# The second part of a hybrid attention layer in the order of a written list: pair scores and four-head values in one run, heads permuted

## The chip, the cores and the metric

The kernel runs on one core of a Trainium2 chip. The metric is the device time of one execution in microseconds (us). The kernel before took 233.28 us (median of three runs, 233.16 to 233.49).

The engines are TensorE (PE in the profile; its weight loads stand apart as PEld), VectorE (DVE), ScalarE (ACT), GpSimd (POOL) and SyncE (SP), which here issues the transfers. Each has its own instruction queue, and they wait for one another through semaphores.

## The reference

One decoder layer on a sequence of 256 tokens of width 1024, in float32. Two attention branches run beside each other, both with eight heads: MLA (branch a: low-rank queries, keys and values; 64 + 32 dimensions per head, the 32 with a rotary key that all heads share) and MoBA (branch b: 64 dimensions per head; with 256 tokens there is only one block, so it is causal attention). Cut to what matters:

```python
mod = silu(c) @ w_ada + b_ada
shift, scale, gate = split(mod, 3)
h = rms_norm(x, g_pre) * (1 + scale) + shift
(q_lat, kv_lat, k_rope, z_mla, q_mb, k_mb, v_mb, z_mb, merge_logits) = split_cols(h @ w_in)
q = rms_norm(q_lat, g_q_lat) @ w_uq              # 8 heads of 64 + 32
kv = rms_norm(kv_lat, g_kv_lat) @ w_ukv          # 8 heads of 64 + 64
q_full, k_full = concat(q_nope, rope(q_pe)), concat(k_nope, broadcast(rope(k_rope)))
o_mla = causal_attention(q_full, k_full, v_mla)
y_mla = (o_mla * silu(z_mla)) @ w_o_mla
o_mb = causal_attention(rope(q_mb), rope(k_mb), v_mb)
y_mb = (o_mb * silu(z_mb)) @ w_o_moba
g_a, g_b = split(sigmoid(merge_logits + b_merge))
y = (g_a * y_mla + g_b * y_mb) @ w_out
out = x + gate * rms_norm(y, g_post)
```

## The kernel before

**Split operands.** Every large matrix product is done with operands cut in two: a rounded high part (`w1`, an ACT copy to float32r) and the rest (`w2`, a DVE subtraction of `w1` from the raw weights, L266 in the profile for both, as the helper `free` is recorded). A product is three matmuls: high by high, high by low, low by high. Weights arrive by DMA in five raw buffers of 1 MB (`RAW`), are cut in pieces of 512 columns by `split_one` (L251), and wait in a ring of five pairs `w1`, `w2` of 1024 columns (`RING`). `pump` (L238) issues the next load on SP as soon as a raw buffer is free.

**First stage**, to about 57.7 us: x is normalized, transposed and modulated to `h1` + `h2`, and MoBA's queries, keys and values are projected. Its order is written out by hand: the strings START, STEP and LAST (L44 to L46) are read token by token (`tokens`, L391), and `ordered` (L78) chains each instruction to the one before on its engine. The helper makes all of it L82 in the profile.

**Second part**, from `lat_mm` on. What the steps are:

- `lat_mm` (L525 to L527): the latent projection, 48 matmuls of 416 columns; `lat_stats`, `lat_evac`, `lat_tr` norm and transpose it. `lat_tr` also copies the shared rotary key to all heads, two copies on POOL and one on DVE (L571).
- `moba_rope`, `moba_tr`: rotary embedding of MoBA's q and k (products on DVE L463 and L466, sums on POOL L467) and their transposes.
- `F` (L431), called "filler": one of 24 projections of 128 output columns (the merge gates and the two SiLU gates), 24 matmuls of 256 columns each (L441 to L443), then a tanh on ACT. A raw buffer feeds two fillers.
- `uq_*`, `ukv_*`, `qpe_tr`: MLA's queries, keys and values from the latents.
- `scores` (L656): q·k for a MoBA pair of heads or one MLA head. A MoBA head has 64 dimensions, so its matmuls use 64 rows of the array, the upper or the lower half; the first query block takes one matmul of 128 columns (L669), the second three of 256 (L677). The softmax follows on DVE and ACT.
- `p_tr` (L696): three transposes of the probabilities, and ACT's copy `pT`.
- `pv` (L705): the values of two heads. Each head writes 64 columns of the array: one matmul of 256 columns (L710) and one of 128 (L714), two passes each. Then u, the product with the SiLU gate, and its cut in two.
- `oproj` (L762): the output projections of a branch, 8 per branch, 12 matmuls each, and the merge `yy` with the gates; for branch a POOL subtracts to get the low part `y2` (L781).
- `ada_gate` (L728): the residual gate, summed on DVE over eight weight tiles 1024 wide (L736, L738), and a bias added on POOL (L741).
- `out_mm`, `out_part` (L866 to L907): the last projection in seven pieces, the post-norm and the stores.

These are called in program order, with `fill` putting one to eight fillers or `oproj("b", m)` between the attention steps. The order on each engine is then decided by the framework's scheduler, which simulates the program and gives each engine the instruction that it finds ready; only first-stage instructions are chained by hand. Splits of coming weights are called by `split_ahead` whenever a ring slot is released.

Of the kernel before, what the change touches and what calls it, by code (L numbers as in the profile page):

```python
# [34 lines left out]
HEAD = 213  # L35
LOADS = "a00 a01 w00 w01 a10 a11 " + " ".join(f"w{j}0 w{j}1 a{j + 1}0 a{j + 1}1" for j in range(1, 7)) + " w70 w71 m"
# [9 lines left out]
LAST = "P0v P1v P2v V P0q P0k P1q P2q P1k P2k"  # L46
POOL_LOW = []
# [15 lines left out]
def hybrid_layer_kernel(ctx: ExitStack, tc: tile.TileContext, x, head, cst, gpost, bgate,  # L63
# [128 lines left out]
    def ada_ab(j):  # L192
# [9 lines left out]
    stream += [(("f", 0), win2[0], 2048, 1), (("f", 1), win2[1], 2048, 1), (("uq",), wuq, 1536, 1),  # L202
               (("ukv",), wukv, 1024, 1)]
    stream += [(("f", i), win2[i], 2048, 1) for i in range(2, 12)]
# [17 lines left out]
    for key, src, n, parts in stream:  # L222
        if key[0] != "w":
            loads.append((key, src, 0, n))
        if key == ("out", 0, 0):
            order.append(("gate", 0))
            splits += [(("gate", 0), ("gate",), 0, a, a + 512) for a in (0, 512)]
# [22 lines left out]

    def split_one():  # L251
        if not splits:
            return False
        u, key, c0, a, b = splits[0]
        if key not in raws or got.get(key, 2048) < c0 + b:
            return False
        if a == 0:
            i = order.index(u)
            if i >= RING and order[i - RING] not in finished:
                return False  # L260
            w1s[u] = rg.tile([P, 1024], FR, name="w1", bufs=RING)
            w2s[u] = rg.tile([P, 1024], FR, name="w2", bufs=RING)
        splits.pop(0)
        r = raws[key][:, c0 + a:c0 + b]
        w = key[0] == "w"
        free = lambda eng, f, *a, **k: f(*a, **k)  # L266
        o = ordered if w else free
        if u == ("w", 0, 0) and a == 0:
            o("V", V.tensor_copy, w1s[u][:, a:b], r)
        else:  # L270
            o("A", act, w1s[u][:, a:b], r, AF.Copy)
        rel = key != ("gate",) and (not splits or splits[0][1] != key)
        if w:
            subs.append((u, key, a, b, r, rel))
            return True
        eng = "G" if (order.index(u), a // 512) in POOL_LOW else "V"
        free(eng, dict(V=V, G=G)[eng].tensor_tensor, w2s[u][:, a:b], r, w1s[u][:, a:b], op=OP.subtract)
        if rel:
            release()
        return True  # L280

    subs = []

    def sub_one():
        u, key, a, b, r, rel = subs.pop(0)
        ordered("V", V.tensor_tensor, w2s[u][:, a:b], r, w1s[u][:, a:b], op=OP.subtract)
        if rel:
            release()

    def split_ahead():  # L290
        while split_one():
            pass

    def weights(u, k=None):
        while any(x[0] == u for x in splits):
            assert split_one(), u
# [5 lines left out]
    def done_with(*us):  # L302
        finished.update(us)
        split_ahead()
# [9 lines left out]
    bR = bank("tr")  # L314

# [75 lines left out]
    def tokens(j, toks):  # L391
        for t in toks.split():
            if t == "s":
                if splits[0][1][0] == "w":
                    assert split_one(), splits[0]
            elif t == "d":
                if subs:
                    sub_one()
# [23 lines left out]
    assert splits[0][1][0] != "w" and not subs and len(vlast) == 2  # L422
    finished.update((("w", KT - 1, 0), ("w", KT - 1, 1)))
    split_ahead()
# [4 lines left out]
    fcount = [0]  # L429

    def F():  # L431
        i = fcount[0]
        if i >= 24:
            return
        fcount[0] += 1
# [35 lines left out]
    mop = {}  # L471
# [3 lines left out]
    def moba_rope(w, t):  # L475
# [3 lines left out]
        r = rr[w][:, t]  # L479
        rope_nat(b, t, 64, 1, r, G)  # L480

    def moba_tr(w, t):
        b = bank("tr")
        for i in range(4):
            nc.tensor.transpose(b[:, i * P:(i + 1) * P], rr[w][:, t, i * P:(i + 1) * P], ident)
        src = b.rearrange("p (k n) -> p k n", k=4)
        if t == 0:
            act(m0[:, w], src, AF.Copy)
        if w:
# [12 lines left out]
    qlat = [sb.tile([P, 256], FT, name=f"qlat{t}") for t in range(2)]  # L502
    kvlat = [sb.tile([P, P], FT, name=f"kvlat{t}") for t in range(2)]
    kpe = sb.tile([P, 2, 32], FT, name="kpe")
    qpe = sb.tile([P, 2, 256], FT, name="qpe")
# [8 lines left out]
    bA = []  # L514

    def lat_mm():
        bA.extend(bank("tr") for _ in range(2))
        for i in range(4):
            key = ("l", i // 2, i % 2)
# [454 lines left out]
```

## Time and profile before

| | us |
|---|---|
| median of three runs | 233.28 |
| profiled execution, its own time | 233.18 |
| its span (first to last instruction) | 231.4 |
| PE busy | 222.5 |
| DVE busy | 169.4 |
| ACT busy | 134.3 |
| POOL busy | 50.8 |
| last matmul starts | 225.29 |

The mean granted TensorE clock was 0.993 of full. The span is some 1.8 us shorter than the execution's own time, which holds the start and the end of the program too. The 231.4 us fall in two: about 58 us for the first stage, and the rest for the second part, with a tail of some 6 us after the last matmul for the norm, the sum and the stores.

A PE record covers a matmul from its first column to a modelled end, so records overlap; the cost of a matmul in a stream is the distance from its start to the next start.

### The profile page before, as it was taken

The numbers are of one execution on the slowest core, as the hardware profiler recorded it, in microseconds if no ns is written. First come the engines' busy times: TensorE is split into PE (matmuls) and PEld (weight loads), VectorE is DVE, ScalarE is ACT, GpSimd is POOL, SyncE is SP. The second block draws the span as 40 slices with busy tenths as digits, with TensorE's granted clock in tenths as the row PEclk, the third lists the DMA queues.
The fourth block names the chain that finished last, engine by engine and source line by source line (L and its number), as shares of the span: only waits on it lengthen the run. The fifth ranks groups of instructions, "written<-read, shape, count | busy, mean of one in ns | idle before, by whom it ended". The sixth has DMA issues, their size and how long they took to land.

```text
span 231.4 us, 4325 instructions
## 1 busy us (share of the span) xinstructions
PE 222.5 (96%) x1578; PEld 191.6 (83%) x1578; DVE 169.4 (73%) x418; ACT 134.3 (58%) x320; POOL 50.8 (22%) x81
## 2 busy tenths in 40 slices
PE   8989999998999999999999999999999999999990
PEld 8846666665899999989879988989998799988890
DVE  1564554444999668989889998799996566899543
ACT  4364555554956668378775986348676534664320
POOL 2188888100045104300000000000400000562000
PEclk9999999999999999999999999999999999999997
DMA  6999998899855904432520536579799710000022
GB/s 249 348 412 406 378 318 307 274 302 331 314 200 181 353 27 170 129 144 74 187 106 13 173 96 244 208 270 302 290 372 416 292 61 0 1 3 0 0 91 91
DMA packets 10247, 47.05 MB, mean 203 GB/s; under 512 B 1137, under 2 KB 1649, under 8 KB 7154
## 3 DMA queue, kind: packets, MB, share of 16 engines
q1 hardware_dynamic: 10226, 46.78, 55.6%
q8 instruction: 12, 0.20, 0.3%
q14 instruction: 9, 0.07, 0.1%
HBM read 45.73 MB, written 1.05 MB: 202 GB/s over the span
## 4 chain that ended last, share of the span: by engine, by line
PE 91%; DVE 2%; issue 2%; ACT 2%; POOL 0%; POOLq 0%; DVEq 0%; ACTq 0%
PE acc L441 9%; PE acc L443 9%; PE acc L442 9%; PE pv L82 8%; PE sc L82 6%; PE acc L82 6%; PE tr L82 5%; PE pv L710 3%; PE acc L769 3%; PE tr L700 3%; PE acc L770 2%; PE acc L771 2%; PE sc L677 2%; PE sc L669 2%; PE sc L893 2%
## 5 line engine op out<-in xcount | busy, mean ns | idle before, releaser
L266 ACT ACTIVATE w<-raw 128x512 fp32r<-128x512 f32 (+1 forms) x93 | 52.3, 617 | 35.7 <-PE acc L442 9.6
L266 DVE TENSOR_TENSOR w<-raw,w 128x512 fp32r<-128x512 f32 (+1 forms) x93 | 63.8, 726 | 6.8 <-ACT w L266 5.8
L441 PE MATMUL acc<-h,w 128*128 128x256 f32 x184 | 53.1, 289 | 0.1
L443 PE MATMUL acc<-h,w 128*128 128x256 f32 x184 | 52.8, 287 | 0.0
L442 PE MATMUL acc<-h,w 128*128 128x256 f32 x184 | 52.3, 284 | 0.0
L441 PEld LDWEIGHTS acc<-h,w 128*128 128x128 f32 x184 | 34.7, 188 | 1.2 <-issue 0.7
L443 PEld LDWEIGHTS acc<-h,w 128*128 128x128 f32 x184 | 34.7, 188 | 0.6
L442 PEld LDWEIGHTS acc<-h,w 128*128 128x128 f32 x184 | 34.7, 188 | 0.3
L82 DVE TENSOR_TENSOR w<-raw,w 128x512 fp32r<-128x512 f32 x24 | 17.1, 732 | 14.0 <-ACT w L82 13.3
L741 POOL TENSOR_TENSOR gacc<-gacc,bgt 1x1024 f32<-1x1024 f32 x1 | 2.6, 2555 | 68.8 <-DMA raw<-in_wo_dram 68.8
L82 PE MATMUL sc<-w,h 128*128 128x512 f32 x48 | 16.6, 426 | 0.8 <-ACT xnT L82 0.5
L82 PE MATMUL pv<-w,h 128*128 128x512 f32 x48 | 15.5, 407 | 1.0 <-ACT w L82 1.0
L781 POOL TENSOR_TENSOR y<-yy,y 128x256 fp32r<-128x256 f32 x8 | 8.5, 1071 | 36.4 <-ACT y L780 36.4
L82 PE MATMUL acc<-w,h 128*128 128x512 f32 x48 | 15.6, 410 | 0.2 <-ACT h L82 0.2
L82 ACT ACTIVATE w<-raw 128x512 fp32r<-128x512 f32 x23 | 13.7, 619 | 1.6 <-DMA raw<-in_win_dram 1.6
L689 ACT ACTIVATE p<-p,mx 128x128 f32<-128x128 f32 (+1 forms) x32 | 14.2, 447 | 0.3 <-DVE mx L686 0.2
L82 PEld LDWEIGHTS sc<-w,h 128*128 128x128 f32 x48 | 8.0, 189 | 5.2 <-issue 2.9
L82 PEld LDWEIGHTS acc<-w,h 128*128 128x128 f32 x48 | 8.5, 188 | 4.3 <-ACT h L82 2.8
L82 PEld LDWEIGHTS pv<-w,h 128*128 128x128 f32 x48 | 8.5, 188 | 4.3 <-ACT w L82 3.0
L467 POOL TENSOR_TENSOR rr<-rr,m 128x512 f32<-128x512 f32 x4 | 5.6, 1420 | 25.6 <-DVE m L466 25.6
L693 DVE TENSOR_SCALAR p<-p,sm 128x128 f32<-128x128 f32 (+1 forms) x32 | 10.8, 380 | 0.1
L82 ACT ACTIVATE h<-xnT,ab 128x256 fp32r<-128x256 f32 x8 | 4.8, 601 | 10.3 <-DVE ab L82 8.8
(255 smaller groups left out, 525.9 us busy)
## 6 DMA issues: line engine op xcount, KB each, us to landing
raw<-in_win_dram SPq DMA_DIRECT2D x12, 1024.0 KB, 5.0
raw<-in_wada_dram SPq DMA_DIRECT2D x16, 512.0 KB, 7.2
raw<-in_win_dram SPq DMA_DIRECT2D x8, 512.0 KB, 7.6
raw<-in_wadag_dram SPq DMA_DIRECT2D x4, 1024.0 KB, 5.2
raw<-in_wo_dram SPq DMA_DIRECT2D x4, 1024.0 KB, 5.0
raw<-in_wout_dram SPq DMA_DIRECT2D x4, 1024.0 KB, 10.2
raw<-in_win_dram SPq DMA_DIRECT2D x8, 256.0 KB, 7.8
raw<-in_winl_dram SPq DMA_DIRECT2D x2, 832.0 KB, 6.9
```

Of the source, the lines that this page charges most:

```text
L82: r = f(*a, **k)
L266: free = lambda eng, f, *a, **k: f(*a, **k)
L441: mm(o, w1[:, k], h1[:, k], start=(k == 0), stop=False)
L442: mm(o, w1[:, k], h2[:, k], start=False, stop=False)
L443: mm(o, w2[:, k], h1[:, k], start=False, stop=(k == KT - 1))
L467: eng.tensor_tensor(dst, dst, m2, op=OP.add)
L689: act(p[:, a:e], p[:, a:e], AF.Exp, scale=scale, bias=mx[:, t:t + 1], accum_out=sm[:, t:t + 1])
L693: V.tensor_scalar(p[:, a:e], p[:, a:e], sm[:, t:t + 1], None, op0=OP.mult)
L700: nc.tensor.transpose(b[:, i * P:(i + 1) * P], p[:, i * P:(i + 1) * P], ident)
L710: mm(b[64 * i:64 * i + 64, 0:S], v[0][:, h * 64:h * 64 + 64], pTt[br, h][:, 0:S], start=True, stop=False, skip_group_check=True)
L769: mm(o, w1[:, k, c0:c0 + P], u1[br][:, k], start=(k == 0), stop=False)
L781: G.tensor_tensor(y2[:, m], yy, y1[:, m], op=OP.subtract)
```

## The change

The second part gets an order written by hand, too. A string PLAN of some 500 tokens names steps; each step is now a Python generator that stops (`yield`) where another engine's part begins, and each further token of the same name runs its next piece. For PE, ACT and DVE the framework's scheduler is switched off (`tc.manual_schedule`): their instructions run in the order in which the tokens issue them. `s` and `d` are the two halves of a weight split (ACT's copy, DVE's subtraction), `F7` a filler, `sb2` the scores of MoBA heads 2 and 3, `sa3` those of MLA head 3, `tb0` a transposition, `vb0` the values of MoBA heads 0 to 3, `A3` and `B3` output projections, `O2` a piece of the last projection, `G` one step of the residual gate.

```diff
+PLAN = """
+R00 s d s R01 L0 R11 d L2 s L3 L1 s d R10 F1 s d ls ls d s ls kr d F0 F0 s q01 q00 q00 d F2 lt q01 s q01 F2 F3
...
+sb4 sb6 tb2 d F12 sb4 tb3 d sb6 F14 tb2 sb6 sb6 s sb4 tb4 sb4 d sa1 F13 sb6 sa0 F14 tb4 sb6 s F14 tb5 tb5 vb0
...
+s B3 s B5 d A0 d B6 A1 A3 x G A0 B7 A1 G A2 A0 A2 B7 A5 d A3 s d A4 A6 A2 s A1 A5 d A3 s s A5 A7 A6 O0 A7 d s
+A6 A4 A4 A7 O1 s d s gg d s O2 d O2 O3 gg s d d O3 d O4 gg O2 O2 O3 O4 O5 O5 O3 O6 O5 O6 O4 O6"""
...
-LAST = "P0v P1v P2v V P0q P0k P1q P2q P1k P2k"
+LAST = "s d P0v P1v P2v V s d s d P0q P0k P1q P2q P1k P2k"
...
+    in_order = tc.manual_schedule(engines={mybir.EngineType.PE, mybir.EngineType.Activation, mybir.EngineType.DVE})
...
+    for tok in PLAN.split():
+        if tok == "s":
+            split_one()
+        elif tok == "d":
+            sub_one()
+        elif tok == "G":
+            ada_gate(nxt["G"])
+            nxt["G"] += 1
+        else:
+            if tok not in gens:
+                gens[tok] = begin(tok)
+            next(gens[tok], None)
+            if tok == "sa7" and not cap[0] == RAW:
+                cap[0] = RAW
+                pump()
```

Splits are 1024 columns wide instead of 512 (832 instead of 416 for the latent weights). The loads of the residual gate's weights go behind those of the output projections, and until the last MLA score only three raw buffers are handed to loads (two hold MLA operands):

```diff
-            cut = size // 2
-            splits += [(key + (i,), key, c0, a, e) for a, e in ((0, min(cut, m)), (cut, m)) if a < m]
-        if key[0] == "f" and key[1] >= 8:
-            loads.append((("g", key[1] - 8), wadag[key[1] - 8], 0, 2048))
-    held, finished = [0], set()
+            cut = 512 if key[0] == "w" else m
+            splits += [(key + (i,), key, c0, a, min(a + cut, m)) for a in range(0, m, cut)]
+        if key[0] in ("ob", "oa"):
+            i = 2 * (key[0] == "oa") + key[1]
+            loads.append((("g", i), wadag[i], 0, 2048))
+    held, finished, cap = [0], set(), [RAW]
...
-        while loads and (loads[0] == "m" or held[0] < RAW or loads[0][0] in raws):
+        while loads and (loads[0] == "m" or held[0] < cap[0] or loads[0][0] in raws):
...
+    cap[0] = RAW - 2
```

The values of four heads are one step, in one bank of 512 columns, with one gate product, one copy and one subtraction of 512 columns behind it:

```diff
-    def pv(br, m):
+    def pv(br, g):
         v = va if br == "a" else vb
         b = bank("pv")
-        for i in range(2):
-            h = 2 * m + i
-            mm(b[64 * i:64 * i + 64, 0:S], v[0][:, h * 64:h * 64 + 64], pTt[br, h][:, 0:S], start=True, stop=False,
+        for n in range(4):
+            h, c0, q = 4 * g + n, S * (n // 2), 64 * (n % 2)
+            mm(b[q:q + 64, c0:c0 + S], v[0][:, h * 64:h * 64 + 64], pTt[br, h][:, 0:S], start=(n < 2), stop=False,
                skip_group_check=True)
-        for i in range(2):
-            h = 2 * m + i
-            mm(b[64 * i:64 * i + 64, P:S], v[1][:, h * 64:h * 64 + 64], pTt[br, h][:, S:384], start=False, stop=True,
+        for n in range(4):
+            h, c0, q = 4 * g + n, S * (n // 2), 64 * (n % 2)
+            mm(b[q:q + 64, c0 + P:c0 + S], v[1][:, h * 64:h * 64 + 64], pTt[br, h][:, S:384], start=False, stop=True,
                skip_group_check=True)
```

The shared rotary key is spread to the heads by three transfers on SP's queue. The gate's bias is added on DVE. The heads of `w_uq` and `w_ukv` are permuted on the host, so that the heads in one half of a bank are neighbours in the destination:

```diff
-        for x, n, e in ((a0[:, 1], P, "G"), (ak1, S, "V"), (aop["k2"], S, "G")):
-            dict(V=V, G=G)[e].tensor_copy(x[pe, 1:H], x[pe, 0:1].to_broadcast([32, H - 1, n]))
+        for x, n in ((ak1, S), (aop["k2"], S), (a0[:, 1], P)):
+            x = x.bitcast(FT)
+            nc.sync.dma_start(x[pe, 1:H], x[pe, 0:1].to_broadcast([32, H - 1, n]))
...
-            G.tensor_tensor(a[0:1], a[0:1], gt["b"], op=OP.add)
+            V.tensor_tensor(a[0:1], a[0:1], gt["b"], op=OP.add)
...
+    nope, rope = [0, 2, 1, 3, 4, 6, 5, 7], [0, 2, 4, 6, 1, 3, 5, 7]
```

Smaller edits: the scores and softmax of a MoBA pair are issued together, the buffers of p, pT and the SiLU gates are 4, 6 and 3 (of two) instead of 3, 4 and 5, and a few copies of MLA's rotary queries go from DVE to ACT.

**What moves on PE.** In the middle of the second part PE's order was this, around the scores of MoBA head 6 (L669 and L677, written to `sc`) and the values of heads 0 and 1 (L710 and L714, written to `pv`); L441 to L443 are a filler, L624 are transposes:

```order
L443 MATMUL acc<-h_189,w_1315 128x256
L441 MATMUL acc<-h_189,w_1314 128x256
L442 MATMUL acc<-h_190,w_1314 128x256
L443 MATMUL acc<-h_189,w_1315 128x256
L669 MATMUL sc<-m_689 128x128
L710 MATMUL pv<-pT,vbt 64x256
L714 MATMUL pv<-pT,vbt 64x128 x2
L624 MATMUL tr<-cstt,qpe 128x128 x4
L677 MATMUL sc<-km_690,qm_872 128x256
L677 MATMUL sc<-km_690,qm_873 128x256
L677 MATMUL sc<-km_943,qm_872 128x256
L443 MATMUL acc<-h_189,w_1315 128x256
```

After the change the scores of a MoBA pair stand in one run (L728 and L731; here between the matmuls of `uq_nope`, L649 to L651):

```order
L651 MATMUL pv<-ql_682,w_915 128x256
L728 MATMUL sc<-m_671 128x128 x2
L731 MATMUL sc<-km_672,qm_911 128x256 x2
L731 MATMUL sc<-km_672,qm_912 128x256 x2
L731 MATMUL sc<-km_980,qm_911 128x256 x2
L649 MATMUL pv<-ql_682,w_914 128x256
```

And the values of heads 0 to 3 (L774 and L778) stand in one run between two transpositions of probabilities (L762):

```order
L762 MATMUL tr<-cstt,p 128x128 x3
L774 MATMUL pv<-pT,vbt 64x256 x4
L778 MATMUL pv<-pT,vbt 64x128 x4
L762 MATMUL tr<-cstt,p 128x128 x3
L435 MATMUL acc<-h_191,w_1483 128x256
```

Every pair's scores were split over one to three places in the order; now each pair has one place, and the four value runs stand where fourteen stood.

**What moves on DVE.** At the end of the second part DVE did its split subtractions (L266, `w<-raw`) in pieces of 512, two per ring slot, between the y products (L778, L779):

```order
L778 SCALAR_TENSOR_TENSOR yy<-tg_687,acc 128x256
L778 SCALAR_TENSOR_TENSOR yy<-tg_687,pv 128x256
L266 TENSOR_TENSOR w_2459<-raw,w_2458 128x512
L779 TENSOR_TENSOR yy<-yy,tg_688 128x256 x2
L266 TENSOR_TENSOR w_2459<-raw,w_2458 128x512
L266 TENSOR_TENSOR w_2501<-raw,w_2500 128x512 x2
```

After the change they are 1024 wide (recorded under the helper, L95), and the gate's last sum and bias (L806, L810) stand among the y products (L859, L860):

```order
L806 SCALAR_TENSOR_TENSOR gacc<-raw,sc,gacc 128x1024
L810 TENSOR_TENSOR gacc<-gacc,bgt 1x1024
L859 SCALAR_TENSOR_TENSOR yy<-tg_669,acc 128x256
L860 TENSOR_TENSOR yy<-yy,tg_670 128x256
L852 SCALAR_TENSOR_TENSOR tg_670<-tg_670,acc 128x256
L95 TENSOR_TENSOR w_2292<-raw,w_2291 128x1024
L859 SCALAR_TENSOR_TENSOR yy<-tg_669,pv 128x256
L860 TENSOR_TENSOR yy<-yy,tg_670 128x256
L95 TENSOR_TENSOR w_2407<-raw,w_2406 128x1024
```

The gate's work, which ended before the output projections of branch a, now lies between them, and a subtraction holds DVE for a whole ring slot at a time.

More of the change, by code (lines that the diff above doesn't have):

```diff
@@ L224, in hybrid_layer_kernel @@
             loads.append((key, src, 0, n))
-        if key == ("out", 0, 0):
+        if key == ("out", 0, 1):
             order.append(("gate", 0))
-            splits += [(("gate", 0), ("gate",), 0, a, a + 512) for a in (0, 512)]
+            splits.append((("gate", 0), ("gate",), 0, 0, 1024))
         size = 2 * NL if key[0] == "l" else 1024
@@ L286, in sub_one @@
         ordered("V", V.tensor_tensor, w2s[u][:, a:b], r, w1s[u][:, a:b], op=OP.subtract)
+        if not any(x[0] == u for x in splits + subs):
+            ready.add(u)
         if rel:
             release()
-    def split_ahead():
-        while split_one():
-            pass
     def weights(u, k=None):
-        while any(x[0] == u for x in splits):
-            assert split_one(), u
+        assert u in ready, u
         w = w1s[u], w2s[u]
@@ L303, in done_with @@
         finished.update(us)
-        split_ahead()
     pump()
@@ L444, in F @@
         done_with(key)
+        fdone.add(i)
+        yield
         kind, m = ORDER[i]
@@ new lines, in lat_tr, with q_evac @@
+        for x, n in ((ak1, S), (aop["k2"], S), (a0[:, 1], P)):
+            x = x.bitcast(FT)
+            nc.sync.dma_start(x[pe, 1:H], x[pe, 0:1].to_broadcast([32, H - 1, n]))
+    def q_evac(parts):
+        q1, q2 = aop["q"][:, 0], aop["q"][:, 1]
+        for p, hs, src in parts:
+            if not p.start:
+                act(a0[p, 0, hs], src[:, :, 0:P], AF.Copy)
+            act(q1[p, hs], src[:, :, P:S], AF.Copy)
+        yield
+        for p, hs, src in parts:
+            if p.start:
+                V.tensor_copy(a0[p, 0, hs], src[:, :, 0:P])
+        for p, hs, src in parts:
+            V.tensor_tensor(q2[p, hs], src[:, :, P:S], q1[p, hs], op=OP.subtract)
@@ new lines, in k_evac, with nope_parts @@
+    def k_evac(parts):
+        for p, hs, src in parts:
+            act(ak1[p, hs], src, AF.Copy)
+        yield
+        for p, hs, src in parts:
+            V.tensor_copy(a0[p, 1, hs], src[:, :, 0:P])
+        for p, hs, src in parts:
+            V.tensor_tensor(aop["k2"][p, hs], src, ak1[p, hs], op=OP.subtract)
+    def nope_parts(b, g):
+        return [(slice(0, 64), slice(4 * g + 2 * i, 4 * g + 2 * i + 2),
+                 b[i * 64:(i + 1) * 64, :].rearrange("p (g n) -> p g n", g=2)) for i in range(2)]
@@ L624, in qpe_tr, with kv_used @@
                 nc.tensor.transpose(b[:, g * S + t * P:g * S + (t + 1) * P], qpe[:, t, g * P:(g + 1) * P], ident)
-        for i in range(4):
-            q_evac((slice(64, 96), slice(i, i + 5, 4)), b[32 * i:32 * i + 32, :].rearrange("p (g n) -> p g n", g=2))
+        yield
+        yield from q_evac([(slice(64, 96), slice(2 * i, 2 * i + 2),
+                            b[32 * i:32 * i + 32, :].rearrange("p (g n) -> p g n", g=2)) for i in range(4)])
+        made.add("aqpe")
+    def kv_used(i):
+        un.add(("kv", i))
+        if all(("kv", k) in un for k in range(4)):
+            done_with(("ukv", 0))
     def ukv_nope(g):
+        assert "kl" in made
         w1, w2 = weights(("ukv", 0))
@@ L773, in oproj @@
             done_with(key)
+        yield
         if br == "b":
+            assert ("tg", 8 + m) in made
             V.scalar_tensor_tensor(tg[1][:, m], tg[1][:, m], 1.0, o, op0=OP.add, op1=OP.mult)
+            made.add(("tb", m))
             return
+        assert ("tg", m) in made and ("tb", m) in made and 23 in fdone
+        if not ys:
+            ys.extend(sb.tile([P, 8, S], FR, name=f"y{i}", tag=f"hy{i}") for i in (1, 2))
         yy = wk.tile([P, S], FT, name="yy", tag="hf", bufs=2)
@@ L895, in out_mm, with out_piece @@
                 done_with(("out", nh, kg, k // 2))
-    banks = [bank("sc") for _ in range(2)]
-    for kg in range(2):
-        for t in range(2):
+    banks = []
+    def out_piece(n):
+        if n < 4:
+            kg, t = divmod(n, 2)
+            if not kg:
+                assert len(banks) == t
+                banks.append(bank("sc"))
+            assert kg == 0 or len(banks) == 2
             out_mm(0, kg, t, banks[t], 0, 512)
             if kg:
-                out_part(t, 0, 512, banks[t])
@@ new lines, in hybrid_layer_kernel @@
+    for tok in PLAN.split():
+        if tok == "s":
+            split_one()
+        elif tok == "d":
+            sub_one()
+        elif tok == "G":
+            ada_gate(nxt["G"])
+            nxt["G"] += 1
+        else:
+            if tok not in gens:
[4 more added lines that the diff above has]
+                pump()
+    assert not (splits or subs or pt) and nxt["G"] == 8
+    left = [tok for tok, g in gens.items() if next(g, "end") != "end"]
@@ L910 @@
+    assert not left, left
+    in_order.__exit__(None, None, None)
 _C_INS = ["head", "cst", "gpost", "bgate", "wada", "wadag", "win1", "winl", "win2", "wuq", "wukv", "wo", "wout"]
```

468 lines of the change are left out of this document (234 added, 234 removed).

## The prediction

> **What bounds the kernel now.** I read the busy shares first, then busy time by stretch, then TensorE's waits, and only then single visits of small matmuls in the timeline.
>
> The page's first part; then busy time in stretches of 20 us (columns: the stretch, then busy us and count of PE, its weight loads PEld, DVE, ACT and POOL, PEclk, DMA share, GB/s); then the list of what PE waited for:
>
> ```profile
> PE 222.5 (96%) x1578; PEld 191.6 (83%) x1578; DVE 169.4 (73%) x418; ACT 134.3 (58%) x320; POOL 50.8 (22%) x81
> ...
> 60.00:80.00 20.00, 20.00 (x133) 19.41 (x131) 17.99 (x40) 13.06 (x33) 6.64 (x5) 1.00 0.69 251
> ...
> 120.00:140.00 20.00, 20.00 (x159) 18.19 (x157) 19.23 (x61) 16.85 (x45) 0.00 (x0) 1.00 0.31 106
> ...
> PE pv L82 <- ACT w L82: 1.0, 1, 1.0
> ```
>
> PE is busy without a gap from 60 us on, and its longest wait, 1.0 us, lies in the first stage, which the change leaves nearly alone. So TensorE sets the pace; a wait taken from another engine is worth nothing, and only TensorE's own time can shrink. The number of matmuls stays the same. What is left is time that PE counts as busy but in which no column streams: a matmul record covers a modelled end, so the true cost is read from one start to the next. DVE is the runner-up, 19.23 of 20 us in one stretch: every microsecond taken from PE there brings DVE nearer.
>
> **The price of a visit.** A MoBA score uses 64 rows of the array, a value product 64 columns; everything around them uses all 128. The timeline of PE (start, us, engine, line, operation, tiles, rows*columns, shape, count) round a one-head score:
>
> ```profile
> 107.75 0.28 PE L441 MATMUL acc<-h,w 128*128 128x256 f32 x1
> 107.87 0.28 PE L442 MATMUL acc<-h,w 128*128 128x256 f32 x1
> 108.08 0.49 PE L669 MATMUL sc<-m 64*128 64x128 f32 x2
> 108.32 0.60 PE L677 MATMUL sc<-km,qm 64*128 64x256 f32 x3
> 108.85 0.39 PE L443 MATMUL acc<-h,w 128*128 128x256 f32 x1
> 109.07 0.28 PE L441 MATMUL acc<-h,w 128*128 128x256 f32 x1
> ```
>
> Full matmuls of 256 columns start .12 us apart (107.75, 107.87; .119 over longer runs). From 107.87 to 109.07 are 1.20 us, in which two full ones take .24: the score costs **.96**. How much of it is entry and exit shows where only a side-by-side pair of matmuls is in the visit:
>
> ```profile
> 98.96 0.28 PE L443 MATMUL acc<-h,w 128*128 128x256 f32 x1
> 99.17 0.39 PE L677 MATMUL sc<-km,qm 64*128 64x256 f32 x2
> 99.49 0.39 PE L441 MATMUL acc<-h,w 128*128 128x256 f32 x1
> 99.71 0.27 PE L442 MATMUL acc<-h,w 128*128 128x256 f32 x1
> ```
>
> .75 less .24 is .51, and the pair's own pass is .12: **.38–.39 per visit** is drain and refill, .58 the content of a score. A pair that starts together costs what one head costs. Two heads one after the other cost more:
>
> ```profile
> 102.32 0.28 PE L443 MATMUL acc<-h,w 128*128 128x256 f32 x1
> ...
> 103.72 0.39 PE L441 MATMUL acc<-h,w 128*128 128x256 f32 x1
> 103.95 0.28 PE L442 MATMUL acc<-h,w 128*128 128x256 f32 x1
> ```
>
> 1.63 less .24 is 1.39. The values in the same way, first the two visits of one pair of heads (the second holds three full transposes of .11 each), then the one place where a whole pair goes at once:
>
> ```profile
> 139.87 0.28 PE L443 MATMUL acc<-h,w 128*128 128x256 f32 x1
> 140.07 0.65 PE L710 MATMUL pv<-pT,vbt 128*64 128x256 f32 x2
> 140.65 0.39 PE L441 MATMUL acc<-h,w 128*128 128x256 f32 x1
> 140.87 0.28 PE L442 MATMUL acc<-h,w 128*128 128x256 f32 x1
> ...
> 141.35 0.28 PE L443 MATMUL acc<-h,w 128*128 128x256 f32 x1
> 141.56 0.43 PE L710 MATMUL pv<-pT,vbt 128*64 128x256 f32 x1
> ...
> 142.66 0.37 PE L441 MATMUL acc<-h,w 128*128 128x256 f32 x1
> 142.86 0.28 PE L442 MATMUL acc<-h,w 128*128 128x256 f32 x1
> ```
>
> ```profile
> 134.64 0.28 PE L442 MATMUL acc<-h,w 128*128 128x256 f32 x1
> 134.85 0.65 PE L710 MATMUL pv<-pT,vbt 128*64 128x256 f32 x4
> ...
> 135.55 0.59 PE L710 MATMUL pv<-pT,vbt 128*64 128x256 f32 x2
> ...
> 136.58 0.28 PE L441 MATMUL acc<-h,w 128*128 128x256 f32 x1
> ```
>
> First visit: 1.00 − .24 = .76. Second: 1.51 − .24 − .33 = .94. At 134.64 to 136.58: 1.94 − .24 − .33 = 1.37 for a whole pair and the first matmul of the next. The whole pair's eight matmuls (the four of 128 columns in the row left out) run from 134.85 to 135.55, .70 with the entry, so about .65 of content where a split pair has .43 + .61; a value visit's overhead is .76 − .43 = .33.
>
> **The change, part by part.** *Scores.* Before, the four MoBA pairs make nine visits, of .62 and .63 (pairs of one kind), .51, 1.39 (heads 2 and 3), and .96 each for heads 4, 5 and 7, and two for head 6 (.39 and .74): 7.2 us together. After, each pair is one visit in which all four matmuls run side by side (the order's rows): 4 × .96 = 3.8. **Saved 3.4.**
>
> *Values.* Before, six pairs in two visits of .76 and .94 (10.3) and two pairs in 1.37 and .94 (2.3): 12.6. After, four visits of two pairs: 4 × (.33 + 2 × .65) = 6.5. **Saved 6.1.** Transposes of probabilities stay at 48 and are full tiles, so their new grouping is worth nothing.
>
> *Side work.* The three broadcasts of the rope keys go from POOL and DVE to SP's queue, the gate's bias from POOL to DVE, part of the q copies to ACT; none of it is on PE. On SP the broadcasts wait for ACT's and DVE's last rope-key writes, and the loads of filler weights f4 and f5 stand behind them; DVE and POOL have no DMA behind it. Cover: f3, uq and ukv are already there.
>
> *What comes back.* With PE some 9.5 us shorter and the same work on DVE, and DVE in a fixed order, new waits appear. These rows give DVE's prices (two groups of the by-shape listing: count, busy, mean ns, idle before; between them timeline rows of DVE and POOL, and two PE starts at 512 columns):
>
> ```profile
> L738 DVE SCALAR_TENSOR_TENSOR gacc<-raw,sc,gacc 128x1024 f32<-128x1024 f32 x7 | 8.9, 1279 | 0.0
> ...
> 74.48 1.28 DVE L266 TENSOR_TENSOR w<-raw,w 128x512 fp32r<-128x512 f32 x2
> 75.68 0.15 DVE L535 TENSOR_SCALAR rsl<-ssl 128x2 f32<-128x2 f32 x1
> ...
> 69.97 4.32 DVE L266 TENSOR_TENSOR w<-raw,w 128x512 fp32r<-128x512 f32 x4
> ...
> 69.53 3.01 POOL L467 TENSOR_TENSOR rr<-rr,m 128x512 f32<-128x512 f32 x2 [3.16 <-DVE m L466]
> ...
> L781 POOL TENSOR_TENSOR y<-yy,y 128x256 fp32r<-128x256 f32 x8 | 8.5, 1071 | 36.4 <-ACT y L780 36.4
> ...
> L779 DVE TENSOR_TENSOR yy<-yy,tg 128x256 f32<-128x256 f32 x8 | 3.4, 431 | 0.1
> ...
> 205.98 0.39 PE L893 MATMUL sc<-w,y 128*128 128x512 f32 x1
> 206.21 0.40 PE L891 MATMUL sc<-w,y 128*128 128x512 f32 x1
> ```
>
> A 512-wide split subtract takes (75.68 − 74.48)/2 = .60 undisturbed, .07 less than its record. The trace has no 1024-wide one. It lies between 1.1 (two of .60 less a shared start) and 1.21 (the 1279 ns of a 1024-wide operation with two large inputs, less .07); I take 1.15, near the second. The bias add on one row of 1024 I price by the same row, 1.2 (it could be as low as .7, were one row cheaper).
>
> (a) *Start.* DVE is busy 17.99 of 20 us in 60:80, and after the change the rope products of the first q half stand ahead of the last latent split. The second filler can find its split late by nothing or by up to .8 (part of one 1.15 subtract and POOL's slowing of it). I take **.3**.
>
> (b) *Handovers* of score and value banks in the fixed order: none now, bound 0 to .6 (a 512-wide u product each at two or three places). **.2**.
>
> (c) *End.* From the first MLA output projection to the fourth output piece PE needs 9 projections × 12 × .119 = 12.9, 48 × .23 = 11.1 and the gate's .9: 24.9. DVE has there ten 1024-wide subtracts (11.5), sixteen y products at .36 (5.8), two gate sums and the bias (3.6), one more tg product (.4), two gate products (1.2): 22.5. That fits, but POOL's eight y subtracts, 1.07 each, now lie all beside it. At 69.97 four subtracts took 4.32 instead of 2.47 (four of .60, and .07) beside 3.01 of POOL, of which 2.57 overlap: 1.85 lost, .72 of the overlap. Of DVE's 22.5 some 18 have two inputs of the same kind, so of POOL's 8.5 about 8.5 × 18/25 = 6.1 meets them, and 4.4 are lost: DVE would need 26.9. **The wait is 0 to 2.0**; the y products come at PE's pace and DVE can fill the time between, so I take half, **1.0**.
>
> The Trainium skill, "SBUF — State Buffer", section "Who interferes with whom", speaks against the change here: it has DVE's second read port shared with GpSimd under an exclusive lock, so that a DVE instruction with two SBUF inputs and a GpSimd instruction exclude each other. The 69.97 row shows the slowing, but not all of POOL's time lost. By that rule of the Trainium skill the end stretch could lose up to POOL's whole 8.5 us on DVE, by the row 4.4; what the first would give is the third rival below.
>
> **Sum.** The execution shown took 233.18 (median of the runs 233.28). 233.18 − 3.4 − 6.1 + .3 + .2 + 1.0 = **225.0**. The tail after the last matmul is left as it is.
>
> **The rivals.**
> 1. *DVE falls behind in several places.* For it: 19.23 of 20 us in 120:140, where PE sheds about 1.2 us. Against it: half as many split subtracts, each under two old ones, and the 2.0 us cast of rope keys gone. Price: .8 + .6 + 2.0 and .4 in 120:140, 3.8 in all: **227.5**.
> 2. *Pairs don't run side by side* in the new longer runs. Scores would cost 4 × 1.39 = 5.6, values 4 × (.33 + 2 × 1.04) = 9.6; saved 1.6 + 3.0, and 1.5 of waits: **230.1**. Against it: the eight matmuls at 134.85.
> 3. *POOL's whole time is lost to DVE at the end*: 22.5 + 8.5 = 31.0 against 24.9, a wait of 6.1: 233.18 − 9.5 + .5 + 6.1 = **230.3**.
> 4. *Slower: the raw buffers.* After the latent weights only three of five raw buffers take weights until the last MLA score, where two hold MLA operands. The rows (loads by kind: KB each, us from issue to landing; and ACT's splits with their idle time):
>
> ```profile
> raw<-in_win_dram SPq DMA_DIRECT2D x12, 1024.0 KB, 5.0
> ...
> L266 ACT ACTIVATE w<-raw 128x512 fp32r<-128x512 f32 (+1 forms) x93 | 52.3, 617 | 35.7 <-PE acc L442 9.6
> ```
>
> A load feeds two fillers, 48 × .12 = 5.7 us of PE. With three buffers, PE starves once a buffer's round (issue, 5.0 of landing, queue, two ACT copies of about 1.1, two subtracts of 1.15) exceeds 17.1. The gain of 8.2 is gone over eight such loads at 1.02 each, that is from a round of 3 × 6.72 = 20.2; at 21 each load adds 1.3, 10.4 in all, and the time is **235.4**. Against it: the parts sum to 9.5, and the fillers are spread among scores, so a load lasts longer than 5.7. ACT now waits for buffers of splits (PE L442), not for loads.
> 5. *The change doesn't do what it says*: the rows of the order show the runs, so only a wait in each gap could undo it; covered by 1.
>
> **Chances.** Forecast .69, rival 1 .17, rival 2 .04, rival 3 .03, rival 4 .05; .02 for a buffer round near the break-even, no change. Faster by over 0.2% (.5 us, what a measurement of this kernel can tell from no change): .69 + .17 + .04 + .03 = .93; same .02; slower .05. The range: all waits at nothing give 223.7, and visits that touch each other may save .3 more, so 223.4; upward it covers the forecast and most of rival 1, 228.3 (DVE's lateness worth 4.6 instead of 1.5). Left out: rivals 2 to 4 and a little of 1, some .2.
>
> **What would show it.** In PE's timeline: four score visits of about .96 and four value visits of about 1.6. In PE's waits: under 1.5 us in the second part, at a filler near 70 us and among the MLA output projections near the end, released by DVE. DVE's busy share should rise to about 76% with some 90 fewer instructions. Value visits over 2 us mean rival 2; waits on DMA during the fillers rival 4; DVE subtracts of 1.7 or more beside POOL, with PE waiting, rival 3. I am wrong if PE's idle time in the second part exceeds 3 us, or if full matmuls get slower than .119 apart.

## The result, and the profile after

The changed kernel takes 227.66 us (median of four runs, 227.32 to 227.81), 0.9756 of the kernel before, 95% interval 0.9739 to 0.9773. The prediction said 225.0 us, 223.4 to 228.3. The profiled execution took 227.81 us, its span is 226.0 us, the granted TensorE clock 0.998. Two executions below in which TensorE ran slower throughout are in no ratio: one of 722 us in the run with copies, and the one of the run with POOL copies (263.01 us, granted clock .755), of which only DVE's and POOL's records are read.

The visits first. PE's timeline of the changed kernel, one pair's scores (counts are records: a score matmul of 128 columns and every value matmul leaves two) and one run of four heads' values:

```profile
96.03 0.28 PE L651 MATMUL pv<-ql,w 128*128 128x256 f32 x1
96.23 0.49 PE L728 MATMUL sc<-m 64*128 64x128 f32 x4
96.47 0.60 PE L731 MATMUL sc<-km,qm 64*128 64x256 f32 x6
97.00 0.39 PE L649 MATMUL pv<-ql,w 128*128 128x256 f32 x1
97.23 0.28 PE L650 MATMUL pv<-ql,w 128*128 128x256 f32 x1
...
133.55 0.49 PE L762 MATMUL tr<-cstt,p 128*128 128x128 f32 x3
133.97 1.08 PE L774 MATMUL pv<-pT,vbt 128*64 128x256 f32 x8
134.89 0.61 PE L778 MATMUL pv<-pT,vbt 128*64 128x128 f32 x8
135.43 0.55 PE L762 MATMUL tr<-cstt,p 128*128 128x128 f32 x3
```

From 96.03 to 97.23 are 1.20, less two full matmuls of .12: .96. The four score visits cost .96, .97, .97 and .92 by the same reading, 3.8 us, and the four value visits 1.60, 1.65, 1.60 and 1.64, 6.5 us. Before, the scores cost 7.2 us and the values 12.7. **The 9.6 us are saved**, as foretold; the execution is only 5.4 shorter.

Then the list of PE's waits in the changed kernel (us in all, times, longest):

```profile
PE tr L485 <- DVE m L465: 1.2, 1, 1.2
PE pv L95 <- ACT w L95: 1.0, 1, 1.0
...
PE tr L485 <- DVE raw L588: 0.3, 1, 0.3
```

The 1.0 is the first stage's, as before. New in the second part are the two at L485, transposes of MoBA's rotated queries and keys; the list counts only part of what they cost, because the modelled end of the matmul before lies in the gap. Starts of PE at the three places where most time went:

```profile
77.12 0.28 PE L437 MATMUL pv<-h,w 128*128 128x256 f32 x1
78.58 1.25 PE L485 MATMUL tr<-cstt,rr 128*128 128x128 f32 x8 [1.18 <-DVE m L465]
79.58 0.36 PE L435 MATMUL acc<-h,w 128*128 128x256 f32 x1
...
86.24 0.60 PE L485 MATMUL tr<-cstt,rr 128*128 128x128 f32 x4
87.15 0.66 PE L485 MATMUL tr<-cstt,rr 128*128 128x128 f32 x4 [0.32 <-DVE raw L588]
...
202.34 0.39 PE L916 MATMUL sc<-w,y 128*128 128x512 f32 x1
202.62 0.50 PE L917 MATMUL sc<-w,y 128*128 128x512 f32 x1
203.22 0.50 PE L918 MATMUL sc<-w,y 128*128 128x512 f32 x1
```

77.12 to 78.58 is 1.46 where .12 is due, and eight transposes to 79.58 take 1.00 where .87 is due: 1.5 us at the queries. At the keys 86.24 to 87.15 is .91 for four transposes, .44 of them due: .5. With .2 at the second filler that is **2.2 us near the start** of the second part. Near 109 us the first value projection starts .3 late, .15 more goes behind a score at 152 us, and **.6 in the last projection**, of which .4 at 202.62 to 203.22. The first stage ended .3 later in this execution than in the one before, and the tail is .2 longer (6.3 against 6.1). 2.2 + .45 + .6 + .5 = 3.8 of the 4.2 us given back; .4 in small gaps are not placed.

What held the queries' transposes is a chain through four engines. They need the two banks that the latent projection still occupies until ACT and DVE have read them; ACT's reading needs the statistics, and DVE's reading comes behind ACT's (its 1.70 us of waiting below). Timeline of DVE, POOL and ACT, changed kernel:

```profile
72.80 1.21 DVE L95 TENSOR_TENSOR w<-raw,w 128x1024 fp32r<-128x1024 f32 x1
73.93 1.25 DVE L543 TENSOR_SCALAR rsl<-ssl 128x2 f32<-128x2 f32 x1
...
75.16 1.21 DVE L95 TENSOR_TENSOR w<-raw,w 128x1024 fp32r<-128x1024 f32 x1
78.08 0.19 DVE L462 TENSOR_TENSOR kpe<-tr,cos 128x32 f32<-128x32 f32 x1 [1.70 <-ACT latt L549]
78.18 0.25 DVE L465 TENSOR_TENSOR m<-tr,ssin 128x16 f32<-128x16 f32 x2
...
78.81 0.24 DVE L465 TENSOR_TENSOR m<-tr,ssin 128x16 f32<-128x16 f32 x2
...
66.95 3.57 POOL L466 TENSOR_TENSOR rr<-rr,m 128x512 f32<-128x512 f32 x2 [0.17 <-DVE m L465]
72.95 2.20 POOL L466 TENSOR_TENSOR rr<-rr,m 128x512 f32<-128x512 f32 x1 [2.43 <-DVE m L465]
75.33 1.95 POOL L545 TENSOR_TENSOR rsl<-rsl,mhalf 128x4 f32<-128x4 f32 x1 [0.17 <-DVE rsl L544]
...
77.31 0.47 ACT L548 ACTIVATE latt<-tr,rsl 128x256 f32<-128x256 f32 x1 [3.94 <-POOL rsl L545]
```

An operation on two columns (L543) takes 1.25 us, until POOL's sum ends at 75.15, and POOL's power on four columns 1.95, past the end of DVE's subtract. DVE's last readings of the two banks end at 78.43 and 79.05, and the transposes into them start .15 us later, four at 78.58 and four at 79.20. The queries' rope sums, all there by 70.52 (the last is in the POOL row of 66.95), had long been ready. The same places in the kernel before:

```profile
75.98 1.04 POOL L537 TENSOR_TENSOR rsl<-rsl,mhalf 128x4 f32<-128x4 f32 x1 [3.44 <-DVE rsl L536]
...
77.06 0.47 ACT L542 ACTIVATE qlat<-tr,rsl 128x256 f32<-128x256 f32 x1 [2.09 <-POOL rsl L537]
...
79.54 0.60 PE L485 MATMUL tr<-cstt,rr 128*128 128x128 f32 x4
```

POOL's power took 1.04, yet ACT began its reading only .25 us sooner than here; but PE came to the transposes only at 79.54, with most of a third filler ahead of them. Now it is ready for them at 77.24.

### The profile page after: what moved, and what is told of

It reads as the page before. It is cut to its first block, busy times and chain, and to the rows that moved or that the text cites. A ratio compares the mean times of both kernels' runs of the same rounds, so it can differ in the third digit from the quotient of the medians.

```text
span 226.0 us, 4161 instructions
## 1 busy us (share of the span) xinstructions
PE 215.1 (95%) x1578; PEld 188.1 (83%) x1578; DVE 163.1 (72%) x359; ACT 129.6 (57%) x273; POOL 49.6 (22%) x78
## 4 chain that ended last, share of the span: by engine, by line
PE 74%; DVE 11%; ACT 4%; DMA 3%; issue 3%; POOL 2%; SPq 1%; POOLq 0%; DVEq 0%; ACTq 0%
PE acc L435 9%; PE acc L437 9%; PE acc L436 9%; PE sc L95 6%; PE acc L95 6%; PE pv L95 5%; PE tr L95 5%; DVE w L95 4%; DMA raw<-in_wada_dram 3%; PE tr L762 3%; PE sc L731 2%; PE pv L774 2%; PE sc L728 2%; DVE yy L859 1%; DVE gacc L806 1%
## 5 line engine op out<-in xcount | busy, mean ns | idle before, releaser
L95 DVE TENSOR_TENSOR w<-raw,w 128x1024 fp32r<-128x1024 f32 (+2 forms) x71 | 74.9, 1076 | 17.0 <-ACT w L95 16.2
L95 ACT ACTIVATE w<-raw 128x1024 fp32r<-128x1024 f32 (+2 forms) x70 | 61.0, 896 | 6.4 <-PE tr L531 3.0
L863 POOL TENSOR_TENSOR y<-yy,y 128x256 fp32r<-128x256 f32 x8 | 9.1, 1143 | 100.4 <-ACT y L862 100.4
L95 PE MATMUL sc<-w,h 128*128 128x512 f32 x48 | 16.6, 426 | 0.8 <-ACT xnT L95 0.5
L95 PE MATMUL pv<-w,h 128*128 128x512 f32 x48 | 15.3, 407 | 1.0 <-ACT w L95 1.0
L95 PE MATMUL acc<-w,h 128*128 128x512 f32 x48 | 15.6, 410 | 0.2 <-ACT h L95 0.2
L740 DVE CUSTOM_DVE_ANT_0 p<-sc,cstt 128x128 f32<-128x128 f32 (+1 forms) x32 | 10.1, 353 | 7.0 <-PE sc L731 7.0
L466 POOL TENSOR_TENSOR rr<-rr,m 128x512 f32<-128x512 f32 x4 | 7.7, 1930 | 26.0 <-PE tr L532 23.4
L95 PEld LDWEIGHTS sc<-w,h 128*128 128x128 f32 x48 | 8.0, 189 | 5.2 <-issue 2.9
L95 PEld LDWEIGHTS pv<-w,h 128*128 128x128 f32 x48 | 8.5, 188 | 4.4 <-ACT w L95 2.9
L95 PEld LDWEIGHTS acc<-w,h 128*128 128x128 f32 x48 | 8.5, 188 | 4.3 <-ACT h L95 2.8
L95 ACT ACTIVATE rws<-tr 128x256 f32<-128x256 f32 x8 | 3.1, 384 | 13.7 <-PE tr L95 13.7
L95 ACT ACTIVATE h<-xnT,ab 128x256 fp32r<-128x256 f32 x8 | 4.8, 601 | 10.2 <-DVE ab L95 8.8
L765 ACT ACTIVATE pT<-tr 128x384 f32<-128x384 f32 x16 | 7.7, 485 | 4.9 <-PE tr L762 4.9
L443 ACT ACTIVATE tg<-acc,bmh 128x256 f32<-128x256 f32 x15 | 7.0, 468 | 5.8 <-PE acc L437 5.7
```

Of the source, the lines that this page charges most:

```text
L95: r = f(*a, **k)
L466: eng.tensor_tensor(dst, dst, m2, op=OP.add)
L740: V.tensor_tensor_reduce(p[:, a:e], b[:, a:e], mask[:, (1 - t) * P:], scale=1.0, scalar=-3e38, op0=OP.add, op1=OP.max, accum_out=mx[:, t:t ...
L765: act(pTt[br, h], b[:, :384], AF.Copy)
L863: G.tensor_tensor(ys[1][:, m], yy, ys[0][:, m], op=OP.subtract)
```

## The experiments

All ratios are to the kernel before, on the same chip; a ratio is uncertain by some .0017, .4 us. The changed kernel itself stands at .9756.

**The statistics first.**

```diff
-...L1 s d R10 F1 s d ls ls d s ls kr d F0 F0
+...L1 s d F1 s d ls ls kr R10 d s ls d F0 F0
```

> Only the order is changed: the latent statistics (two small DVE operations, POOL's power, ACT's evacuations) and the rotary of the shared key come ahead of the last MoBA rope product and of two split subtracts on DVE. Theory 1 (TensorE waits 1.3 us near 77 us for the latent banks, whose release hangs on a chain DVE-POOL-ACT-DVE that DVE and POOL lengthen for each other): the power falls beside small operations and takes about 1.0 us instead of 1.95, the wait goes, and the time is 226.2 us (225.7 to 226.8). Rival (the transposes wait for the rope sums themselves, or DVE's queue is simply too long there): the last rope sum is now later, the wait stays or grows, 227.5 to 229.

226.05 us, .9676 (.9660 to .9692). DVE and POOL there:

```profile
72.47 0.16 DVE L543 TENSOR_SCALAR rsl<-ssl 128x2 f32<-128x2 f32 x1
...
72.77 1.04 POOL L545 TENSOR_TENSOR rsl<-rsl,mhalf 128x4 f32<-128x4 f32 x1 [2.45 <-DVE rsl L544]
...
73.85 0.47 ACT L548 ACTIVATE latt<-tr,rsl 128x256 f32<-128x256 f32 x1 [0.68 <-POOL rsl L545]
```

And PE, where the wait was:

```profile
76.91 0.28 PE L437 MATMUL pv<-h,w 128*128 128x256 f32 x1
77.03 1.03 PE L485 MATMUL tr<-cstt,rr 128*128 128x128 f32 x8
```

ACT's reading begins 3.5 us earlier, and the transposes start without a gap. So the wait was for the banks; it is the largest part given back. The run moves the statistics and DVE's own reading of the banks (`kr`) forward together; how much each of the two gave it does not show. The last rope sum is later here, but it is a sum of keys (`R10`) and says nothing of the queries: that their sums were not waited for is shown by the POOL row of 66.95 above.

**The pair's heads one after the other.** The score matmuls of a pair, `for i in heads` outside instead of inside the loop over the four products.

> In each of the four score visits the two heads' matmuls are issued one head after the other instead of alternating; visits and everything else stay. Theory 1 (heads in the two halves of the array run together only when they alternate): each visit costs 1.39 us instead of .96, 4 x .43 = 1.7 more, 229.4 us. Rival (only the number of visits counts): no change, 227.7.

228.84 us, .9805 (.9781 to .9828). PE's timeline:

```profile
95.98 0.28 PE L651 MATMUL pv<-ql,w 128*128 128x256 f32 x1
96.18 0.59 PE L728 MATMUL sc<-m 64*128 64x128 f32 x3
...
96.63 0.60 PE L730 MATMUL sc<-km,qm 64*128 64x256 f32 x5
97.17 0.39 PE L649 MATMUL pv<-ql,w 128*128 128x256 f32 x1
97.39 0.28 PE L650 MATMUL pv<-ql,w 128*128 128x256 f32 x1
```

A visit takes 1.41 − .24 = 1.17, not 1.39; the four cost 4.7 instead of 3.8. Of 1.1 us by the ratios .9 is seen. Alternating the heads is worth half of what I priced. The other half lies in the row the price was read from, the visit at 102.32 in the kernel before:

```profile
102.97 0.62 PE L677 MATMUL sc<-km,qm 64*128 64x256 f32 x5
```

Its matmuls come in the same pattern as here, but from the start of this last group to the next full matmul (103.72) are .75 us where this run needs .54 (96.63 to 97.17): PE stood still for part of it, for a reason that stays open. So .2 of the 9.6 us saved was a pause and not the price of a visit.

**Each value run cut in two.**

```diff
+        for half in range(2):
+            for t, d0, d1, p0, p1 in ((0, 0, S, 0, S), (1, P, S, S, 384)):
+                for n in (2 * half, 2 * half + 1):
...
+            if half == 0:
+                yield
```

In the list each value step gets one more token, and a small step (`tb6`, `sa4`, `ta5`, `B2`) stands between the two halves of each run.

> Each run of four heads' values is cut in two visits of a pair each, with full matmuls or transposes between them; scores, splits and the rest stay (two small steps are moved to lie between). Theory 1 (a fixed price for each entry into the half array): 4 x .33 = 1.3 more, 229.0 us, eight visits of about 1.0 us. Rival (entry is hidden beside transposes, only the pairs' own passes cost): 227.7 to 228.1.

229.68 us, .9831 (.9815 to .9847): 1.8 us by the ratios. The eight visits cost .95 to 1.00, but for one:

```profile
175.21 0.87 PE L776 MATMUL pv<-pT,va 128*64 128x256 f32 x8
176.41 0.38 PE L844 MATMUL acc<-u1b,w 128*128 128x256 f32 x1 [0.34 <-DVE tg L852]
...
177.99 0.87 PE L776 MATMUL pv<-pT,va 128*64 128x256 f32 x8
178.79 0.38 PE L844 MATMUL acc<-u1b,w 128*128 128x256 f32 x1
```

There PE waits .4 for a bank that DVE still reads. The eight visits come to 8.3 us, 8.3 − 6.5 = 1.8, of which 1.4 are four more entries at .35. The entry price holds, beside transposes as well.

**Low parts of y on DVE.**

```diff
-        G.tensor_tensor(ys[1][:, m], yy, ys[0][:, m], op=OP.subtract)
+        (G if m < 2 else V).tensor_tensor(ys[1][:, m], yy, ys[0][:, m], op=OP.subtract)
```

> Six of the eight low parts of y are subtracted on DVE instead of POOL. Theory 1 (while POOL works on two inputs DVE stands still for POOL's own time of some .75 us, so .34 on DVE itself is cheaper): DVE's stretch near the end gets shorter by up to 6 x .4 = 2.4 us, TensorE's .6 us of waits in the last projection go, 227.1 us. Rival (DVE is only slowed a little by POOL and is already the late engine there): DVE gets 6 x .34 = 2.0 us more, and the time is 228.3 to 229.7.

230.04 us, .9849 (.9832 to .9866), 2.2 us slower than the changed kernel by the ratios: the rival was right in its direction, and a little more came than it said. PE's waits near the end grew from .6 to 2.7, the longest in this row:

```profile
203.31 0.50 PE L916 MATMUL sc<-w,y 128*128 128x512 f32 x1
205.24 0.50 PE L917 MATMUL sc<-w,y 128*128 128x512 f32 x1 [1.43 <-DVE w L95]
```

The split subtracts are not lengthened any more (the gate's takes 1.22 instead of 1.77, the three behind it 3.49 instead of 4.59: 1.7 us won). But the six operations take 2.4 us, and DVE waits .5 for ACT's y and 1.1, instead of .6, for POOL to free the buffer of a y product. So the three subtracts begin at 203.97 instead of 201.35. POOL cost DVE less there than its whole time.

**Rope sums on DVE.** `rope_nat(b, t, 64, 1, rr[w][:, t], V)` instead of `G`.

> The changed kernel, with the four sums of MoBA's rotary embedding on DVE instead of POOL; order and all else stay. Theory 2 (DVE and POOL exclude each other while both have two inputs in SBUF: in 64 to 75 us DVE loses 1.2 us in two subtracts and 1.1 us in one tiny operation to POOL's sums): the four sums cost DVE 4 x .60 = 2.4 us and give 2.3 us back, the latent statistics come at the same time, 227.4 to 228.0 us, and the lengthened DVE records are gone. Rival (DVE's lengthened records are not POOL's doing): DVE is 2.4 us later there, TensorE waits 1.3 to 2.4 us more, 229 to 230.

228.15 us, .9765 (.9742 to .9787): no change. The lengthened records are gone from DVE:

```profile
69.77 2.35 DVE L95 TENSOR_TENSOR w<-raw,w 128x1024 fp32r<-128x1024 f32 x2
...
75.16 0.16 DVE L543 TENSOR_SCALAR rsl<-ssl 128x2 f32<-128x2 f32 x1
...
75.48 1.94 POOL L545 TENSOR_TENSOR rsl<-rsl,mhalf 128x4 f32<-128x4 f32 x1 [34.22 <-DVE rsl L544]
```

The two subtracts had taken 3.56 in the changed kernel, the L543 operation 1.25. Its successor begins at 75.23, against 75.09 there, and the first rope product of this execution was .5 us earlier: DVE is .6 us behind with 2.4 us more work, so it is held up some 1.8 us less. POOL's power comes no sooner and is as long as before, beside the split subtract that follows the statistics, so the banks come free no earlier. PE's wait is now split, 1.1 at the second filler and 1.1 at the queries' transposes.

**Splits in halves.** Each 1024-wide (832-wide) copy and subtract as two of 512 (416).

> The changed kernel with each split of 1024 (832) columns issued as two halves on ACT and on DVE, as the kernel before had them, in the same order. Theory 1 (the wide splits only save the start of an operation): DVE has some 46 x .07 = 3.2 us more work in the second part, ACT some 7 us, and where DVE is full (60 to 80, 180 to 210 us) about a third of it lands on TensorE: 228.7 us (228.2 to 229.5). Rival (the long subtracts are what holds POOL up; halves let it in earlier): POOL's power at 75 us ends .5 us earlier and TensorE waits less, 226.9 to 227.4.

228.74 us, .9796 (.9778 to .9813), about 1 us slower. PE waits .5 at the second filler, 1.6 at the queries, .8 in the last projection, a little more at each place where it waited already, and .3 and .2 at two new ones (175.9 and 132.0 us). The rival was half right: POOL's power took 1.42 instead of 1.95, but DVE came to the statistics later, and it ended at 77.41, no sooner than the 77.28 of the changed kernel.

**Copies instead of transfers** for the shared key.

> The changed kernel with the three broadcasts of the shared rotary key as copies on POOL (two) and DVE (one), as before, instead of transfers on SP's queue. Theory 1: DVE is held 2.0 us near 87 us, where it idles 1.2 us, so splits come .8 us later and TensorE waits 0 to .8: 227.7 to 228.5 us. Rival (the transfers, which wait on SP with two weight loads behind them, are what makes splits late): faster than the changed kernel, 226.8 to 227.4.

227.80 us, .9745 (.9729 to .9761): no change; no trace of this run is read. The transfers on SP neither cost nor gave time that can be measured.

**More moves of the same kind.**

```diff
-lt F1 lt s d q10 lt lt q11 d q10
+lt F1 lt lt lt s d q10 q11 d q10
...
-F8 un1 v0 d s F9 v0 v1 un2
+F8 un1 d s F9 v0 v0 v1 un2
...
-O0 A7 d s A6 A4 A4 A7 O1
+O0 A7 s A6 A4 d A4 A7 O1
```

> The order of the run with the statistics first, and three more moves by the same reading: the shared key's pieces ahead of a split subtract (TensorE's .5 us at the k transposes), one filler ahead of the first value projection (.3 us), and the last y product ahead of the gate's split subtract (.4 us at the third output piece). Theory 1 (these waits are what is left of the given-back time): 226.05 - 1.2 = 224.9 us (224.5 to 225.5). Rival (each of them only moves the wait to the next filler): 225.8 to 226.3.

227.11 us, .9713 (.9692 to .9733): 1 us slower than with the statistics alone, and slower than even the rival had it. The first move did what it should, the .5 at the keys is gone. The others only moved their waits; PE's list has

```profile
PE acc L435 <- ACT tg L443: 0.6, 1, 0.6
...
PE sc L917 <- DVE w L95: 0.5, 1, 0.5
```

the one behind the moved filler, whose tanh on ACT now stands behind more work, the other in the last projection, where the gate's subtract had been moved into the way of the weights' subtracts.

**Only the first of them.**

> The order with the statistics first and, of the three further moves, only the shared key's pieces ahead of a split subtract. Theory 1 (TensorE's .5 us at the k transposes goes and nothing is late behind it; the other two moves of the last run made the new waits of .8 and .6 us): 226.05 - .5 = 225.6 us (225.2 to 225.9). Rival (that move made one of the new waits): 226.0 to 226.8.

225.68 us, .9669 (.9652 to .9685), some 2 us below the changed kernel and faster than both kernels. In its trace the .5 at the keys is gone; against the order with the statistics alone (.9676) the .2 us by the ratios are less than the uncertainty.

**The last two low parts on DVE**, behind a subtract, on top of that.

> The same, and the low parts of the last two y products on DVE, behind the split subtract that follows them, instead of POOL. Theory 2 (three subtracts beside two POOL operations take 4.6 us instead of 3.5; two operations of .34 on DVE take less): DVE is .4 us earlier for the gate products, y is ready earlier, TensorE's .4 us at the third output piece go: .4 less than the run beside it, 225.2 us. Rival (DVE waits there for ACT's y, as it did when six of them were moved): equal or up to .5 more.

225.69 us, .9665 (.9647 to .9684): equal. The wait at the third output piece fell from .36 to .21, and the three subtracts there take 3.6 us instead of 4.58, with .75 for the two low parts between them; nothing of it can be measured in the time.

**POOL copies.** POOL's subtract of y replaced by a copy; the low part of y is left out of the computation.

> The changed kernel in which POOL copies the y product instead of subtracting its high part from it (the low part is left out of the computation, POOL's operation has one input instead of two). In the changed kernel DVE's gate sum at 187 us takes 1.76 instead of 1.28, the gate's split 1.77 instead of 1.22 and three subtracts 4.59 instead of 3.49 beside POOL. Theory 2a (only two inputs on both sides exclude each other): those records fall back to 1.28, 1.22 and 3.49. Theory 2b (any POOL operation on SBUF holds DVE up): they stay longer by POOL's own time.

The records of DVE and POOL:

```profile
225.19 1.22 DVE L95 TENSOR_TENSOR w<-raw,w 128x1024 fp32r<-128x1024 f32 x1
...
227.91 1.22 DVE L95 TENSOR_TENSOR w<-gacc,w 128x1024 fp32r<-128x1024 f32 x1
...
225.34 1.33 POOL L863 CAST y<-yy 128x256 fp32r<-128x256 f32 x1 [0.60 <-DVE yy L860]
227.27 0.40 POOL L863 CAST y<-yy 128x256 fp32r<-128x256 f32 x1 [0.59 <-DVE yy L860]
```

A POOL copy takes .40 beside DVE products that read one input from a bank, and 1.33 beside a DVE subtract with both inputs in SBUF: it, too, waits for DVE, and ends .26 after the subtract's end (226.67 against 226.41). DVE's records are nearly normal (1.22; three were 1.28 to 1.30 and a pair 2.55 instead of 2.35). That is what theory 2a foretold for DVE, but its reason fails, since POOL's copy has one input and waits all the same. Theory 2b, every record longer by POOL's time, is not what DVE shows: here POOL came second and did the waiting. So the holding-up falls on whichever comes second, as it fell on DVE at L543 in the changed kernel; whether a copy that comes first would hold DVE for its .40 this run does not show.

## Why the prediction came out as it did

**The price of a visit: right.** Entry of .38 and .33, contents of .58 and .65 gave 3.8 and 6.5 us for the eight new visits; measured 3.8 and 6.5. Cutting the value runs again brought 1.4 us in entries back. Only the price of two heads one after the other, in the second rival, was too high (1.39 assumed, with a pause of .2 in it; 1.17 measured).

**(a) Start: the step that failed.** I took .3 us, with .8 as the bound, and looked at DVE's split for the second filler. That cost .2. The wait came one step further, 2.0 us at the transposes of queries and keys, 2.2 in all. At the queries, 1.5 of it, PE waited for banks that the latents' statistics and DVE's pieces hold, and at the keys, .5, for the bank from which the shared key was still being read (gone where those pieces come earlier). The row for it was in the trace of before: ACT began reading those banks at 77.06, and PE reached the transposes at 79.54. The new order puts them one filler earlier, and I had checked the order for splits but not for banks. Shown by the run with the statistics first, which takes the chain 3.5 us forward and the wait away.

**(b) Handovers:** .2 taken, .45 measured, inside the bound of .6.

**(c) End:** 1.0 taken out of 0 to 2.0, .6 measured. DVE's records there are about 2.1 us longer beside POOL, not 4.4: .5 in the gate sum at 187 us, .5 in the gate's split, 1.1 in three subtracts. Another .6 DVE waited at 193 us for POOL to free one of the two buffers of the y product, a wait that my sum did not have. I had charged POOL's recorded 1.07 per operation, but that record holds POOL's own waiting for DVE; undisturbed the subtract takes .73 to .86.

**Tail and first stage:** taken as unchanged; .2 and .3 later in the profiled execution.

**Sum:** 233.18 − 9.6 + 2.2 + .45 + .6 + .2 + .3 = 227.3, the execution took 227.81. The miss of the median, 2.7 us, is the 1.9 of (a) above all. That the time still fell into the range is in part luck: the range was drawn wide enough for the first rival, and the chain that took most of the room is in none of the rivals.

**The rivals.** The time is that of the first rival, DVE late in several places, to .2 us, but not by its sum: DVE's lateness near the end and in 120:140 was small (PE without a wait in 120:140), and what stood for it was the chain at the start. Rival 2 is out: heads ran side by side. Rival 3, POOL's whole time lost to DVE, is out as a price. Its mechanism holds better than my row had it. That a DVE instruction with two SBUF inputs and a GpSimd instruction that reads SBUF exclude each other is what the Trainium skill says in "SBUF — State Buffer", "Who interferes with whom"; these traces agree, with a POOL operation of 1.04 lasting 1.95 past the end of DVE's subtract. A DVE operation of .16 with one tensor input also lasted 1.25 until POOL ended; it is a `tensor_scalar`, which the same section of the Trainium skill counts among those that can take the shared ports. That section of the Trainium skill says as well that the instruction that comes second is the one that blocks; that fits, since here each engine waited in turn. So DVE does not lose all of POOL's time, and to read the rule as DVE's loss alone, as I did, was the mistake in that rival's price. Rival 4 is out, no wait of PE on a transfer lies in the second part.

**The signs named ahead:** the eight visits came as described. PE's waits, read from start to start, were 3.2 us in the second part and not under 1.5, at the transposes more than at a filler, and near the end in the last projection instead of among the output projections. The sign of being wrong, over 3 us of idle time of PE there, is met by this reading and not by the records, which leave 1.75 us free (161.70 less 159.95 busy, 58 to 219.7 us), because their modelled ends cover part of each wait. DVE's share went down, not up: 72%, 163.1 us instead of 169.4. Its split subtracts alone take 74.9 us instead of 80.9, 71 wide ones for 117 narrow ones; there are 59 instructions fewer, not 90.

## What to carry to other kernels

Where TensorE has no waits, its time still holds the price of every change between whole and half tiles, .33 to .38 us a visit here; count the visits, from start to start, and put them in one place. When a hand-written order makes an engine arrive earlier, look for every resource that it takes at that place, banks first, and when the last reader lets it go; an order checked for data alone misses that. Move the head of a long chain through small operations ahead of big ones on the same engine: one such move gave 1.6 us (1.9 by the ratios), more than any change of engine.

## What was unexpected

DVE and POOL held each other up far more than in the kernel before: a two-column DVE operation took 1.25 us instead of .15, POOL's 512-wide sums 1.93 us on average instead of 1.42. Moving the work to the other engine did not help, neither with four rope sums (no change) nor with six y subtracts (2.2 us slower).
